# Strassen tiles with A11 and A12 split ahead of the sums, and a pause of the modulation's dot products

## The chip, the cores and the metric

The kernel runs on one core of one Trainium2 chip. The metric is the device time of one execution in microseconds (us); a kernel is judged by the median of several executions. The core has TensorE (PE in the profile, PEld its weight loads), VectorE (DVE), ScalarE (ACT), GpSimd (POOL) and SyncE (SP, which issues the DMAs here).

## The reference, cut to what matters

One inference step of two layers over 128 context and 512 latent tokens, D_MODEL = 1024, D_FF = 2816, all in float32. Each layer is a feed-forward network (FFN), a mixer (attention in layer 0, Fourier mixing in layer 1) and a second FFN, each with a shift, a scale and a gate that come from a modulation:

```python
def _modulation(cond, w, b):
    m = jax.nn.silu(cond) @ w + b            # w: 1024 x 9*1024 per layer
    return jnp.split(m, N_MOD, axis=-1)      # N_MOD = 9

def _swiglu(h, wg, wu, wd):
    return (jax.nn.silu(h @ wg) * (h @ wu)) @ wd

hp = _modulate(_rms(yp, norm_g[l, 0]), mp[0], mp[1])
hs = _modulate(_rms(ys, norm_g[l, 0]), ms[0], ms[1])
yp = yp + 0.5 * mp[2] * _swiglu(hp, ffn_wg[l, 0], ffn_wu[l, 0], ffn_wd[l, 0])
ys = ys + 0.5 * ms[2] * _swiglu(hs, ffn_wg[l, 0], ffn_wu[l, 0], ffn_wd[l, 0])
...                                          # mixer, then the second FFN with m[6], m[7], m[8]
```

There are four FFNs: (0,0), (0,1), (1,0) and (1,1), by layer and place. The last one, (1,1), is followed by the final norm and the outputs.

## The kernel before, in words

**Float32 by three products.** Weights and activations are split into a high part `hi` (cast to fp32r) and a low part `lo` (the rest), and each product is three matmuls, hi by hi, hi by lo and lo by hi (`mm3`, L560, whose three matmuls are L565, L566 and L567). Weights come from HBM raw by SP's queue (`raw`), are cast to `whi` and get their `wlo` by a subtraction. In the first three FFNs ACT casts (L131) and POOL subtracts (L134); in the last FFN ACT casts (L160) and DVE subtracts (L163).

**The first three FFNs** (`ffn`, L874). The 2816 hidden columns are 22 tiles of 128, worked off in chunks: `CHUNKS = (4, 4, 2, 4, 4, 4)`. The tokens are two halves, half 0 of 384 and half 1 of 256 columns. A chunk first makes gate and up of its tiles for both halves (`products`, then the scaling by the norm at L812 and the bias at L822), then `down` (L855) runs the down products of the chunk for half 0 and then for half 1. For each of the eight blocks d of x, `down` takes a PSUM bank, runs the matmuls and has DVE add the product, times the gate, to x (`add_x`, L776). The one-bank PSUM tiles are named `t` (four), the two-bank ones `s` (two). A four-tile chunk has 12 matmuls for each block, the two-tile chunk (chunk 2) has 6, so there a bank is filled in half the time while the add takes as long.

**Modulation.** The 9 vectors of each layer are dot products on DVE that are spread over the FFNs: a task (`mods`, L663) loads 512 KB of w_mod into one of two buffers `wmt` and makes two dots of 128x1024 with it (L681, in the profile CUSTOM_DVE_ANT_0 and a read of the accumulator, out `junk` and `mod`, in `junk<-wmt,crow`). The order of all work is fixed when the kernel is built. The program keeps a clock of its own (`now`, in units it calls ns) that `tick` moves on after each product, and a task goes on when the clock has reached its `wake`. Between two dots the task yields its pace: 2600 for vector 2 of layer 0, 3800 for the other vectors of layer 0, 4300 for layer 1. `need_mod` finishes what a step needs at once.

**The last FFN** (`ffn_last`, L1008) runs chunk 0 as before and chunks 1 to 5 by Strassen's scheme: 18 tiles. A tile's weight is a 2x2 matrix of blocks: rows gate (A11, A12) and up (A21, A22), columns the two halves of K. The 640 tokens are two halves of 320, `first` and `second`. Seven products make the four results instead of eight, each of them 12 matmuls of 128x320, 84 in all (`seven`, L927):

```
P1 = A11 B11   P2 = A12 B21   P6 = S2 T2   P7 = S3 T3   P5 = S1 T1   P3 = S4 B22   P4 = A22 T4
S1 = A21 + A22,  S2 = S1 - A11,  S3 = A11 - A21,  S4 = A12 - S2      (weights)
```

in the order 1, 2, 6, 7, 5, 3, 4 (in a chunk's last tile 1, 2, 6, 5, 7, 3, 4), where the first two products of a tile are drawn between the last ones of the tile before it. The forms of B and T are made once from the norm's output.

**The weights' forms of a tile** are made by a task `load_sums` (L179). It loads two raws of 128x1024, `r1` = (A11, A12) and `r2` = (A21, A22). `take_turn` keeps the tasks in order, and `self.live` lets only two tiles have sums at one time. DVE makes the sums, S1 in the place of A21, ACT casts them (`form`, L192) and DVE makes their low parts (L196). `whole` (L155) makes the high and low part of a whole raw, 128x1024, into a pair of weight buffers:

```python
for c in halves:                                   # L159
    nc.scalar.copy(hi[:, c], raw[:, c])            # L160
yield self.pace
for c in halves:
    nc.vector.tensor_tensor(lo[:, c], raw[:, c], hi[:, c].bitcast(F32), op=ALU.subtract)   # L163
```

`whole(r1)` gives A11 and A12, `whole(r2)` gives S1 and A22. A pair of buffers is taken when `u.room` is above 0 (`take_grain`, six pairs in all); `seven` gives room back after the products that used a pair last, `ffn_last` after the downs. In chunks 1 to 5 `pin` (L996) fixes the program order of PE, DVE and ACT, so each of them works off its instructions as they were written. After a chunk's products its down products run, for half `second` and then `first`.

Of the kernel before, what the change touches and what calls it, by code (L numbers as in the profile page):

```python
# [37 lines left out]
RAW = 1024  # L38
# [49 lines left out]
class Units:  # L88
# [89 lines left out]
    def load_sums(self, ap):  # L178


        k, nc = self.k, self.k.nc
        W = RAW // 2
        r1 = k.raw()
        r2 = k.wide(k.rawpool, "raw", F32, RAW) if self.turn % 2 else k.raw()
        nc.sync.dma_start(r1, ap[:, :RAW])
        nc.sync.dma_start(r2, ap[:, RAW:])
        forms = {}
        tt = nc.vector.tensor_tensor

        def high(name, src):  # L190
            forms[name] = tuple(k.wide(k.fpool, "form", w=W) for _ in range(2))
            nc.scalar.copy(forms[name][0], src)  # L192

        def low(name, src):
            h, l = forms[name]
            tt(l, src, h.bitcast(F32), op=ALU.subtract)  # L196

        yield from self.take_turn(3500)
        while self.live > 1:
            yield 300  # L200
        self.live += 1
        s3, s2 = (k.wide(k.spool2, "s", F32, W) for _ in range(2))
        s1, a11, a12 = r2[:, :W], r1[:, :W], r1[:, W:]
        tt(s3, a11, s1, op=ALU.subtract)
        tt(s1, s1, r2[:, W:], op=ALU.add)
        yield self.pace
        high("S3", s3)
        tt(s2, s1, a11, op=ALU.subtract)
        yield self.pace
        high("S2", s2)  # L210
        low("S3", s3)
        yield self.pace
        low("S2", s2)
        tt(s2, a12, s2, op=ALU.subtract)
        yield self.pace
        high("S4", s2)
        h, l = yield from self.whole(r1)
        forms["A11"], forms["A12"] = (h[:, :W], l[:, :W]), (h[:, W:RAW], l[:, W:RAW])
        low("S4", s2)
        yield self.pace  # L220
        h, l = yield from self.whole(r2)
        forms["S1"], forms["A22"] = (h[:, :W], l[:, :W]), (h[:, W:RAW], l[:, W:RAW])
        yield self.pace
        self.served_one()
        return forms
# [225 lines left out]
class Kern:  # L451
# [422 lines left out]
    def ffn(self, l, i, nrm, nxt, begin=None):  # L874
# [3 lines left out]
        u = self.units  # L878
        for ch, nf in enumerate(CHUNKS):
            last = ch == len(CHUNKS) - 1  # L880
# [9 lines left out]
            first = gm == (0, 2) and ch == 0  # L890
            if not first:
                self.need_mod(gm)
            self.down(wds, gA, 0, gate, nxt if last else None, gm if first else None)
            self.down(wds, gB, 1, gate, nxt if last else None)
            u.prefetch(nf // 2)
# [28 lines left out]
            if not all and steps[1:]:  # L924
                self.staged.append(steps[1:])

    def seven(self, w, forms, G, last):  # L927


        nc = self.nc  # L930
        u = self.units
# [25 lines left out]
        for p in (1, 2, 6, 5, 7, 3, 4) if last else (1, 2, 6, 7, 5, 3, 4):  # L957
            new = ()
# [3 lines left out]
            elif p == 2:  # L962
                c = self.bank()[:, :NH]
                product(c, "A12", "B21", True)
                u.room += 1
                tt(t["s1"], c, t["s1"], op=ALU.add)
                new = (lambda: nc.scalar.activation(t["s1"], t["s1"], AF.Silu),)
            elif p == 6:
# [13 lines left out]
                new = (lambda: tt(gate, t["s3"], gate, op=ALU.mult), *split(gate, "second"))  # L982
            else:
                product(b, "A22", "T4", False)
                u.room += 1
                tt(t["s2"], b, t["s2"], op=ALU.add)
                tt(t["s2"], t["s2"], t["s1"], op=ALU.mult)
                new = split(t["s2"], "first")
# [25 lines left out]
    def ffn_last(self, l, i, nrm, nxt, before_last):  # L1014
# [3 lines left out]
        u = self.units  # L1018
        wide = lambda n: [tuple(self.wide(self.gpool, "g") for _ in range(2)) for _ in range(n)]
        for ch, nf in enumerate(CHUNKS):  # L1020
# [14 lines left out]
            else:  # L1035
# [3 lines left out]
                gs = wide(nf)  # L1039
                old = None  # L1040
                for n, G in enumerate(gs):
                    new = self.seven(u.get(), nrm.forms, G, n == nf - 1)
                    for step in (new, new, old, new, old, new, new) if n else [new] * 5:
                        next(step)
                    old = new
# [585 lines left out]
    def run(self):  # L1631
# [49 lines left out]
        paces = {}  # L1681
        for l in range(2):
            for m in range(2 if l == 0 else 0, NMOD):
                paces[l, m] = 2600 if (l, m) == (0, 2) else (3800 if l == 0 else 4300)
                for d in range(KT):
                    self.modq.append((l, m, d))
        self.modtask = Task(self, self.mods(paces))
# [285 lines left out]
```

## Time and profile before

| | |
|---|---|
| three executions | 2335.15, 2340.88 (median), 2344.72 us |
| profiled execution | 2336.35 us, its span 2334.6 us |
| busy: PE, PEld | 2272.8 us (97%), 2242.2 us (96%) |
| busy: DVE, ACT, POOL | 1609.9 us (69%), 821.4 us (35%), 795.8 us (34%) |
| DMA | 243.92 MB, mean 104 GB/s |

The trace is that of one execution, the profiled one. Times in it count from the span's start. The first three FFNs and the mixers take up to about 1840 us, then come the last FFN with its Strassen chunks and the tail. In a row of the timeline the bracket at its end is the time for which the engine stood idle before the instruction, and what released it. "x12" is a count of instructions or, in a timeline, of equal neighbours that were put together. The page's "granted clock" (PEclk) is the mean of TensorE's clock over a stretch, 1.00 being 2.4 GHz and 0.50 being 1.2 GHz.

### The profile page before, as it was taken

The numbers are of one execution on the slowest core, as the hardware profiler recorded it, in microseconds if no ns is written. First come the engines' busy times: TensorE is split into PE (matmuls) and PEld (weight loads), VectorE is DVE, ScalarE is ACT, GpSimd is POOL, SyncE is SP. The second block draws the span as 40 slices with busy tenths as digits, with TensorE's granted clock in tenths as the row PEclk, the third lists the DMA queues.
The fourth block names the chain that finished last, engine by engine and source line by source line (L and its number), as shares of the span: only waits on it lengthen the run. The fifth ranks groups of instructions, "written<-read, shape, count | busy, mean of one in ns | idle before, by whom it ended". The sixth has DMA issues, their size and how long they took to land.

```text
span 2334.6 us, 38917 instructions
## 1 busy us (share of the span) xinstructions
PE 2272.8 (97%) x15518; PEld 2242.2 (96%) x15518; DVE 1609.9 (69%) x3113; ACT 821.4 (35%) x1725; POOL 795.8 (34%) x655
## 2 busy tenths in 40 slices
PE   8999999999999999999999999999999999999998
PEld 6999999998899999999999999999999999999998
DVE  5867877767677776777666767676457586667665
ACT  4222222254545632222224322222237343333434
POOL 1444444464111244353445533533346530000002
PEclk9999999999999999999999999999999999999999
DMA  8444434421111233444433334443221221322212
GB/s 301 153 128 135 143 127 146 138 76 58 33 42 37 82 100 127 127 144 127 126 118 109 109 121 132 130 132 127 73 75 64 64 73 55 99 63 80 85 46 73
DMA packets 70469, 243.92 MB, mean 104 GB/s; under 512 B 7888, under 2 KB 12688, under 8 KB 70032
## 3 DMA queue, kind: packets, MB, share of 16 engines
q1 hardware_dynamic: 70288, 241.44, 32.3%
q8 instruction: 122, 2.00, 0.4%
q14 instruction: 59, 0.48, 0.1%
HBM read 238.62 MB, written 2.79 MB: 103 GB/s over the span
## 4 chain that ended last, share of the span: by engine, by line
PE 83%; DVE 9%; ACT 3%; issue 2%; POOL 1%; DMA 1%; SPq 0%; POOLq 0%; ACTq 0%; DVEq 0%
PE s L567 16%; PE s L566 16%; PE s L565 16%; PE t L565 11%; PE t L566 11%; PE t L567 11%; DVE x L776 1%; DVE junk L681 1%; DVE b L822 1%; ACT whi L131 1%; PE t L1316 1%; POOL wlo L134 1%; DVE dg L620 0%; DVE sm L1259 0%; DVE b L575 0%
## 5 line engine op out<-in xcount | busy, mean ns | idle before, releaser
L134 POOL TENSOR_TENSOR wlo<-raw,whi 128x512 fp32r<-128x512 f32 x484 | 683.6, 1443 | 991.7 <-ACT whi L131 695.1
L131 ACT CAST whi<-raw 128x1024 fp32r<-128x1024 f32 (+1 forms) x249 | 251.4, 1035 | 508.1 <-PE t L566 293.7
L565 PE MATMUL s<-a,whi 128*128 128x386 f32 (+1 forms) x1188 | 403.1, 340 | 1.7 <-ACT a L286 0.8
L567 PE MATMUL s<-a,wlo 128*128 128x386 f32 (+1 forms) x1188 | 403.1, 339 | 0.1
L566 PE MATMUL s<-a,whi 128*128 128x386 f32 (+1 forms) x1188 | 402.3, 339 | 0.0
L681 DVE CUSTOM_DVE_ANT_0 junk<-wmt,crow 128x1024 f32<-128x1024 f32 x256 | 343.0, 1340 | 2.3 <-ACT crow L1697 0.3
L776 DVE SCALAR_TENSOR_TENSOR x<-t,mod,x 128x128 f32<-128x128 f32 (+2 forms) x640 | 247.9, 423 | 138.5 <-PE t L567 136.4
L565 PE MATMUL s<-b,whi 128*128 128x256 f32 (+1 forms) x1056 | 297.0, 281 | 0.2 <-DVE a L812 0.2
L566 PE MATMUL s<-b,whi 128*128 128x256 f32 (+1 forms) x1056 | 296.8, 281 | 0.0
L567 PE MATMUL s<-b,wlo 128*128 128x256 f32 (+1 forms) x1056 | 296.7, 281 | 0.0
L565 PE MATMUL t<-a,whi 128*128 128x384 f32 (+1 forms) x660 | 225.3, 342 | 3.9 <-ACT a L574 3.0
L565 PE MATMUL t<-b,whi 128*128 128x256 f32 x760 | 216.7, 285 | 10.6 <-DVE x L776 6.3
L565 PEld LDWEIGHTS s<-a,whi 128*128 128x128 f32 x1188 | 224.2, 189 | 2.8 <-ACT a L286 0.9
L567 PEld LDWEIGHTS s<-a,wlo 128*128 128x128 f32 x1188 | 224.2, 189 | 2.2 <-issue 1.6
L566 PEld LDWEIGHTS s<-a,whi 128*128 128x128 f32 x1188 | 224.3, 189 | 1.6 <-issue 1.2
L566 PE MATMUL t<-a,whi 128*128 128x384 f32 (+1 forms) x660 | 224.7, 341 | 0.3 <-DVE a L575 0.2
L567 PE MATMUL t<-a,wlo 128*128 128x384 f32 (+1 forms) x660 | 224.2, 340 | 0.0
L567 PE MATMUL t<-b,wlo 128*128 128x256 f32 x760 | 214.1, 282 | 0.0
L566 PE MATMUL t<-b,whi 128*128 128x256 f32 x760 | 214.1, 282 | 0.0
L565 PEld LDWEIGHTS s<-b,whi 128*128 128x128 f32 x1056 | 199.0, 188 | 0.7 <-issue 0.5
L566 PEld LDWEIGHTS s<-b,whi 128*128 128x128 f32 x1056 | 199.1, 189 | 0.0
L567 PEld LDWEIGHTS s<-b,wlo 128*128 128x128 f32 x1056 | 198.8, 188 | 0.0
(307 smaller groups left out, 4761.4 us busy)
## 6 DMA issues: line engine op xcount, KB each, us to landing
raw<-in_gu SPq DMA_DIRECT2D x176, 512.0 KB, 3.7
wmt<-in_wm SPq DMA_DIRECT2D x134, 512.0 KB, 3.7
raw<-in_dn SPq DMA_DIRECT2D x88, 512.0 KB, 3.7
raw<-in_uq SPq DMA_DIRECT2D x8, 512.0 KB, 3.7
raw<-in_wo SPq DMA_DIRECT2D x8, 512.0 KB, 3.6
raw<-in_fw SPq DMA_DIRECT2D x8, 512.0 KB, 3.8
crow<-in_wm SPq DMA_DIRECT2D x6, 512.0 KB, 5.8
junk<-in_wm SPq DMA_DIRECT2D x4, 512.0 KB, 5.8
```

Source lines behind the costliest of these rows:

```text
L131: nc.scalar.copy(hi, raw[:, :e])
L134: eng.tensor_tensor(lo[:, c], raw[:, c], hi[:, c].bitcast(F32), op=ALU.subtract)
L565: mm(out, wh, xh, start=first and i == 0, stop=False)
L566: mm(out, wh, xl, start=False, stop=False)
L567: mm(out, wl, xh, start=False, stop=last and i == end)
L681: nc.vector.tensor_tensor_reduce(self.junk, raw, self.crow[:, c * D : (c + 1) * D], 1.0, 0.0, ALU.mult, ALU.add, self.mod[l][m][:, d, c : ...
L776: self.mark = self.nc.vector.scalar_tensor_tensor(xd, ps[:, cols], gate[:, d, c : c + 1], xd, ALU.mult, ALU.add)
L822: nc.vector.scalar_tensor_tensor(g[:, cols], up[:, cols], bias[:, 1, c : c + 1], g[:, cols], ALU.add, ALU.mult)
L1316: nc.tensor.transpose(ps[:, o : o + P], ps2[i][:, kt * P : (kt + 1) * P], self.ident)
```

## The change

The change has three parts. In `load_sums`, `whole(r1)` is called as soon as the task has its turn, ahead of the wait for `self.live` and of the sums, and the pause that stood behind A11's split now stands ahead of S4's low part. The room for the weight buffers is counted for that order: `seven` gives one after product 2 only in a chunk's first tile, and two after product 4 but for the last tile, where it gives one. In `ffn`, ahead of the downs of a two-tile chunk, the task of the dots is put off until 20000 on the program's clock from there. And the paces of the dots go from 3800 to 3500 in layer 0 and from 4300 to 4000 in layer 1.

```diff
--- before.py
+++ after.py
@@ -196,6 +196,8 @@
             tt(l, src, h.bitcast(F32), op=ALU.subtract)
 
         yield from self.take_turn(3500)
+        h, l = yield from self.whole(r1)
+        forms["A11"], forms["A12"] = (h[:, :W], l[:, :W]), (h[:, W:RAW], l[:, W:RAW])
         while self.live > 1:
             yield 300
         self.live += 1
@@ -214,10 +216,8 @@
         tt(s2, a12, s2, op=ALU.subtract)
         yield self.pace
         high("S4", s2)
-        h, l = yield from self.whole(r1)
-        forms["A11"], forms["A12"] = (h[:, :W], l[:, :W]), (h[:, W:RAW], l[:, W:RAW])
+        yield self.pace
         low("S4", s2)
-        yield self.pace
         h, l = yield from self.whole(r2)
         forms["S1"], forms["A22"] = (h[:, :W], l[:, :W]), (h[:, W:RAW], l[:, W:RAW])
         yield self.pace
@@ -890,6 +890,8 @@
             first = gm == (0, 2) and ch == 0
             if not first:
                 self.need_mod(gm)
+            if nf == 2:
+                self.modtask.wake = max(self.modtask.wake, self.now + 20000)
             self.down(wds, gA, 0, gate, nxt if last else None, gm if first else None)
             self.down(wds, gB, 1, gate, nxt if last else None)
             u.prefetch(nf // 2)
@@ -924,7 +926,7 @@
             if not all and steps[1:]:
                 self.staged.append(steps[1:])
 
-    def seven(self, w, forms, G, last):
+    def seven(self, w, forms, G, first, last):
 
 
         nc = self.nc
@@ -962,7 +964,7 @@
             elif p == 2:
                 c = self.bank()[:, :NH]
                 product(c, "A12", "B21", True)
-                u.room += 1
+                u.room += first
                 tt(t["s1"], c, t["s1"], op=ALU.add)
                 new = (lambda: nc.scalar.activation(t["s1"], t["s1"], AF.Silu),)
             elif p == 6:
@@ -982,7 +984,7 @@
                 new = (lambda: tt(gate, t["s3"], gate, op=ALU.mult), *split(gate, "second"))
             else:
                 product(b, "A22", "T4", False)
-                u.room += 1
+                u.room += 1 if last else 2
                 tt(t["s2"], b, t["s2"], op=ALU.add)
                 tt(t["s2"], t["s2"], t["s1"], op=ALU.mult)
                 new = split(t["s2"], "first")
@@ -1039,7 +1041,7 @@
                 gs = wide(nf)
                 old = None
                 for n, G in enumerate(gs):
-                    new = self.seven(u.get(), nrm.forms, G, n == nf - 1)
+                    new = self.seven(u.get(), nrm.forms, G, n == 0, n == nf - 1)
                     for step in (new, new, old, new, old, new, new) if n else [new] * 5:
                         next(step)
                     old = new
@@ -1681,7 +1683,7 @@
         paces = {}
         for l in range(2):
             for m in range(2 if l == 0 else 0, NMOD):
-                paces[l, m] = 2600 if (l, m) == (0, 2) else (3800 if l == 0 else 4300)
+                paces[l, m] = 2600 if (l, m) == (0, 2) else (3500 if l == 0 else 4000)
                 for d in range(KT):
                     self.modq.append((l, m, d))
         self.modtask = Task(self, self.mods(paces))
```

What this does to the order of the instructions is shown at three places. Names carry the number of the buffer and of its writing; lines behind L198 are two higher in the kernel after, `ffn`'s and later ones more.

**ACT, the second tile of chunk 1.** The rows begin in the middle of the tile and end where the third tile's first product is drawn in. `raw_3277` is (A11, A12) of the third tile in both, `raw_3278` its other raw. Before:

```order
L948 COPY a_3316_21271<-s_3315_21258 128x320
L967 ACTIVATE a_3316_21271<-a_3316_21271 128x320
L981 ACTIVATE a_3318_21300<-s_3303_21169 128x320
L948 COPY a_3321_21319<-s_3315_21258 128x320
L192 CAST form_3322_21324<-s_3319_21305 128x512
L953 CAST g_3295_21161<-a_3318_21300 128x320
L192 CAST form_3325_21344<-s_3320_21306 128x512
L953 CAST g_3295_21161<-a_3310_21222 128x320
L948 COPY a_3327_21374<-s_3315_21258 128x320
L192 CAST form_3328_21377<-s_3320_21306 128x512
L160 CAST whi_3330_21380<-raw_3277_21020 128x512 x2
L160 CAST whi_3332_21387<-raw_3278_21021 128x512 x2
```

After (`raw_3313` is the fourth tile's (A11, A12), `raw_3248` the second tile's second raw):

```order
L160 CAST whi_3311_21248<-raw_3248_20847 128x512 x2
L160 CAST whi_3316_21262<-raw_3277_21020 128x512 x2
L950 COPY a_3318_21275<-s_3315_21258 128x320
L969 ACTIVATE a_3318_21275<-a_3318_21275 128x320
L983 ACTIVATE a_3320_21306<-s_3295_21152 128x320
L950 COPY a_3323_21325<-s_3315_21258 128x320
L192 CAST form_3324_21330<-s_3321_21311 128x512
L955 CAST g_3287_21144<-a_3320_21306 128x320
L192 CAST form_3327_21350<-s_3322_21312 128x512
L955 CAST g_3287_21144<-a_3304_21208 128x320
L950 COPY a_3329_21380<-s_3315_21258 128x320
L192 CAST form_3330_21383<-s_3322_21312 128x512
```

The casts of `raw_3277` have moved from behind the third tile's last form (`form_3328`) to ahead of the second tile's first copy (`a_3318<-s_3315`), and `raw_3278`'s stay behind the last form.

**DVE, FFN (0,1), the downs of the two-tile chunk.** `x0` to `x7` are the blocks of x; adds of 128x384 are half 0, pairs of 128x128 half 1. ISA rows with `junk` are dots, those with `mod` alone read the sum. Before:

```order
L776 SCALAR_TENSOR_TENSOR x3_78<-t_1991_11506,mod0_8_100,x3_78 128x384
L681 ISA junk_1720_9414,mod1_1_102<-wmt_1721_9415,crow_1719_9413 128x1024
L681 ISA mod1_1_102 128x1
L776 SCALAR_TENSOR_TENSOR x4_79<-s_1992_11514,mod0_8_100,x4_79 128x384
L776 SCALAR_TENSOR_TENSOR x5_80<-s_1993_11526,mod0_8_100,x5_80 128x384
L776 SCALAR_TENSOR_TENSOR x6_81<-t_1994_11534,mod0_8_100,x6_81 128x384
L776 SCALAR_TENSOR_TENSOR x7_82<-t_1995_11545,mod0_8_100,x7_82 128x384
L776 SCALAR_TENSOR_TENSOR x0_75<-t_1996_11553,mod0_8_100,x0_75 128x128 x2
L681 ISA junk_1720_9414,mod1_1_102<-wmt_1721_9415,crow_1719_9413 128x1024
L681 ISA mod1_1_102 128x1
L776 SCALAR_TENSOR_TENSOR x1_76<-t_1997_11562,mod0_8_100,x1_76 128x128 x2
L776 SCALAR_TENSOR_TENSOR x2_77<-t_1998_11573,mod0_8_100,x2_77 128x128 x2
```

After:

```order
L776 SCALAR_TENSOR_TENSOR x3_78<-t_1991_11506,mod0_8_100,x3_78 128x384
L776 SCALAR_TENSOR_TENSOR x4_79<-s_1992_11514,mod0_8_100,x4_79 128x384
L776 SCALAR_TENSOR_TENSOR x5_80<-s_1993_11525,mod0_8_100,x5_80 128x384
L776 SCALAR_TENSOR_TENSOR x6_81<-t_1994_11533,mod0_8_100,x6_81 128x384
L776 SCALAR_TENSOR_TENSOR x7_82<-t_1995_11544,mod0_8_100,x7_82 128x384
L776 SCALAR_TENSOR_TENSOR x0_75<-t_1996_11552,mod0_8_100,x0_75 128x128 x2
L776 SCALAR_TENSOR_TENSOR x1_76<-t_1997_11561,mod0_8_100,x1_76 128x128 x2
L776 SCALAR_TENSOR_TENSOR x2_77<-t_1998_11570,mod0_8_100,x2_77 128x128 x2
L776 SCALAR_TENSOR_TENSOR x3_78<-t_1999_11579,mod0_8_100,x3_78 128x128 x2
L776 SCALAR_TENSOR_TENSOR x4_79<-t_2000_11588,mod0_8_100,x4_79 128x128 x2
L776 SCALAR_TENSOR_TENSOR x5_80<-t_2001_11597,mod0_8_100,x5_80 128x128 x2
L776 SCALAR_TENSOR_TENSOR x6_81<-t_2002_11606,mod0_8_100,x6_81 128x128 x2
```

The two dots between the adds are gone; the next one stands behind the last add of half 1.

**DVE, last FFN, the down of the two-tile chunk.** L204, L205 and L208 (L206, L207 and L210 after) are sums of the next chunk's first tile, L163 the low parts of its A11 and A12, L196 the low part of a form. Pairs of 128x192 and 128x128 are adds of half `second`, 128x320 those of `first`. Before:

```order
L776 SCALAR_TENSOR_TENSOR x5_80<-s_3466_22319,mod1_8_109,x5_80 128x128
L208 TENSOR_TENSOR s_3465_22311<-raw_3440_22142,raw_3439_22141 128x512
L776 SCALAR_TENSOR_TENSOR x6_81<-t_3467_22328,mod1_8_109,x6_81 128x192
L776 SCALAR_TENSOR_TENSOR x6_81<-t_3467_22328,mod1_8_109,x6_81 128x128
L776 SCALAR_TENSOR_TENSOR x7_82<-t_3470_22341,mod1_8_109,x7_82 128x192
L776 SCALAR_TENSOR_TENSOR x7_82<-t_3470_22341,mod1_8_109,x7_82 128x128
L196 TENSOR_TENSOR form_3469_22333<-s_3464_22310,form_3468_22332 128x512
L776 SCALAR_TENSOR_TENSOR x0_75<-t_3471_22350,mod1_8_109,x0_75 128x320
L776 SCALAR_TENSOR_TENSOR x1_76<-t_3474_22362,mod1_8_109,x1_76 128x320
L196 TENSOR_TENSOR form_3473_22355<-s_3465_22311,form_3472_22354 128x512
L214 TENSOR_TENSOR s_3465_22311<-raw_3439_22141,s_3465_22311 128x512
L776 SCALAR_TENSOR_TENSOR x2_77<-t_3475_22370,mod1_8_109,x2_77 128x320
```

After:

```order
L776 SCALAR_TENSOR_TENSOR x7_82<-t_3468_22337,mod1_8_109,x7_82 128x192
L776 SCALAR_TENSOR_TENSOR x7_82<-t_3468_22337,mod1_8_109,x7_82 128x128
L163 TENSOR_TENSOR wlo_3467_22329<-raw_3440_22156,whi_3466_22328 128x512 x2
L206 TENSOR_TENSOR s_3470_22352<-raw_3440_22156,raw_3441_22157 128x512
L207 TENSOR_TENSOR raw_3441_22157<-raw_3441_22157 128x512
L776 SCALAR_TENSOR_TENSOR x0_75<-t_3469_22346,mod1_8_109,x0_75 128x320
L776 SCALAR_TENSOR_TENSOR x1_76<-t_3472_22360,mod1_8_109,x1_76 128x320
L210 TENSOR_TENSOR s_3471_22353<-raw_3441_22157,raw_3440_22156 128x512
L776 SCALAR_TENSOR_TENSOR x2_77<-t_3473_22368,mod1_8_109,x2_77 128x320
L776 SCALAR_TENSOR_TENSOR x3_78<-t_3476_22380,mod1_8_109,x3_78 128x320
L196 TENSOR_TENSOR form_3475_22373<-s_3470_22352,form_3474_22372 128x512
L776 SCALAR_TENSOR_TENSOR x4_79<-t_3477_22388,mod1_8_109,x4_79 128x320
```

Low parts of A11 and A12 and two sums now stand together between the last add of `second` and the first of `first`; before, the sums were drawn between the adds of `second` and the low parts came near the end of `first`.

PE's and POOL's orders are the same before and after. SP's differs in the places of some loads, and there are 256 dots in both.

## Rows read from the trace of the kernel before

**Rows 1.** The page, busy time of each engine (share of the span), number of instructions
```profile
PE 2272.8 (97%) x15518; PEld 2242.2 (96%) x15518; DVE 1609.9 (69%) x3113; ACT 821.4 (35%) x1725; POOL 795.8 (34%) x655
```
**Rows 2.** Waits of PE: line waited for, us in total, times, longest us
```profile
PE s L565 <- ACT whi L160: 12.7, 8, 1.6
PE t L565 <- DVE x L776: 10.4, 11, 2.3
```
**Rows 3.** Timeline of PE at a tile boundary: start, us, engine, line, operation
```profile
1967.76 0.30 PE L567 MATMUL s<-sum,wlo 128*128 128x320 f32 x1
1969.61 0.41 PE L565 MATMUL s<-h,whi 128*128 128x320 f32 x1 [1.55 <-ACT whi L160]
```
**Rows 4.** Timeline of ACT there
```profile
1968.42 0.62 ACT L192 CAST form<-s 128x512 fp32r<-128x512 f32 x1
1968.94 2.18 ACT L160 CAST whi<-raw 128x512 fp32r<-128x512 f32 x4
```
**Rows 5.** Windows: length, busy us (instructions) of each engine, PEclk, DMA share, GB/s
```profile
core 0: us, PE busy (x) PEld busy (x) DVE busy (x) ACT busy (x) POOL busy (x), PEclk, DMA share, GB/s
2068.70:2092.70 24.00, 24.00 (x165) 24.00 (x164) 12.32 (x23) 7.50 (x17) 0.00 (x0) 1.00 0.13 44
1967.76:1971.93 4.17, 2.46 (x16) 1.93 (x14) 3.40 (x7) 3.02 (x6) 0.00 (x0) 1.00 0.08 7
1982.37:1986.58 4.21, 2.44 (x16) 1.92 (x15) 3.39 (x7) 3.81 (x8) 0.00 (x0) 1.00 0.02 2
```
**Rows 6.** Groups of DVE, 1946.77 to 2000.5: count, busy us, mean ns, idle before
```profile
L163 DVE TENSOR_TENSOR wlo<-raw,whi 128x512 fp32r<-128x512 f32 x20 | 12.9, 684 | 1.4 <-ACT whi L160 1.4
L196 DVE TENSOR_TENSOR form<-s,form 128x512 fp32r<-128x512 f32 x7 | 4.8, 683 | 0.0
L954 DVE TENSOR_TENSOR g<-a,g 128x320 fp32r<-128x320 f32 x6 | 2.8, 483 | 0.0
L205 DVE TENSOR_TENSOR raw<-raw 128x512 f32<-128x512 f32 x2 | 1.4, 692 | 0.1
```
**Rows 7.** Windows, two stretches after tile boundaries
```profile
2096.10:2099.40 3.30, 3.30 (x14) 3.30 (x13) 1.60 (x3) 0.46 (x2) 0.00 (x0) 0.50 0.60 171
2276.95:2280.30 3.35, 3.35 (x15) 3.35 (x14) 2.34 (x4) 1.33 (x4) 0.00 (x0) 0.50 0.71 223
```
**Rows 8.** Timelines of PE and DVE, last FFN, down of chunk 2
```profile
2060.92 0.68 DVE L204 TENSOR_TENSOR s<-raw,raw 128x512 f32<-128x512 f32 x1
2064.82 0.38 PE L565 MATMUL t<-g,whi 128*128 128x320 f32 x1 [2.26 <-DVE x L776]
```
**Rows 9.** Windows, half-1 downs of the three two-tile chunks, and 96 gate-up matmuls
```profile
244.46:252.99 8.53, 6.46 (x50) 5.94 (x50) 8.53 (x24) 0.24 (x1) 0.00 (x0) 1.00 0.40 123
1029.20:1037.88 8.68, 6.54 (x50) 5.96 (x49) 8.68 (x25) 0.22 (x1) 0.00 (x0) 1.00 0.42 131
1501.00:1508.43 7.43, 6.29 (x50) 5.91 (x49) 7.43 (x23) 0.23 (x1) 0.00 (x0) 1.00 0.39 133
1009.39:1020.74 11.35, 11.35 (x98) 11.35 (x97) 7.91 (x13) 4.53 (x9) 4.78 (x4) 1.00 0.37 124
```
**Rows 10.** Windows, line L681 alone: DVE busy (dots and their reads), PEclk, DMA, GB/s
```profile
244.46:252.99 8.53, 2.43 (x4) 1.00 0.40 123
1029.20:1037.88 8.68, 2.44 (x4) 1.00 0.42 131
1501.00:1508.43 7.43, 1.29 (x4) 1.00 0.39 133
```
**Rows 11.** Timeline of PE in the second of these downs
```profile
1032.88 0.38 PE L565 MATMUL t<-b,whi 128*128 128x256 f32 x1 [1.74 <-DVE x L776]
```
**Rows 12.** Windows, 60 us of four-tile chunks in FFN (0,0) and FFN (1,0)
```profile
120.00:180.00 60.00, 60.00 (x412) 60.00 (x411) 41.24 (x64) 19.07 (x32) 28.93 (x20) 1.00 0.45 140
1320.00:1380.00 60.00, 60.00 (x416) 60.00 (x415) 45.00 (x77) 13.65 (x24) 21.01 (x16) 1.00 0.40 124
```
**Rows 13.** Dots: duration ns (least/median/longest); and a slow one in the timeline
```profile
L681 DVE CUSTOM_DVE_ANT_0 junk<-wmt,crow x256: 1205/1217/2405, 56.7 to 1642.0; 128x1024 f32<-128x1024 f32 x128
1022.59 2.20 DVE L681 CUSTOM_DVE_ANT_0 junk<-wmt,crow 128x1024 f32<-128x1024 f32 x1
```

## The prediction, made before the change was timed

> **What bounds the kernel now.** I read the engines' busy line first: PE is busy for 2272.8 of 2334.6 us [rows 1], so a change of instructions on another engine is worth what it takes out of PE's 62 us of idle time, out of the slow start after a wait, and out of stretches at the low clock. Then the waits of PE: eight times an `s` product of the last FFN waits for ACT's `whi` of L160, 12.7 us in all, and eleven times a `t` product waits for DVE's `x` of L776, 10.4 us [rows 2]. The timelines show what stands behind each.
>
> At the boundary of two Strassen tiles PE issues the last S1 matmul at 1967.76, and A11's first one only at 1969.61, after 1.55 us of waiting for ACT [rows 3]. ACT casts the form of S4 at 1968.42, and only then, in one run of four casts from 1968.94, A11|A12's and S1|A22's raw weights (L160) [rows 4]. A11|A12 stands behind the sums of its own tile in ACT's order, and so it comes last before it is used first. This happens at tiles 3 and 4 of each of the four four-tile chunks, which are the eight waits.
>
> **Edit 1: A11 and A12 before the sums.** A stretch of 24 us without a stall has 165 matmuls of 128x320 in 24.00 us, 0.146 us each [rows 5]. From the last S1 matmul to the end of A11's twelve are 13 matmuls, 1.90 us. The two boundaries shown took 4.17 and 4.21 us [rows 5], 2.27 and 2.31 over that; the part that is pure wait is 12.7/8 = 1.59. The order now has the two casts of tile T+1's A11|A12 in tile T's first products, ahead of T's first copy out, with five or more products of twelve matmuls (8.8 us) still to run before they are used, and the raw weights' load is the only thing they wait for. I take the whole excess: 8 x 2.29 = 18.3 us. Lower bound, if only the idle time goes: 12.7; upper bound 18.4 (8 x 2.31).
>
> What is late next? In a tile DVE has, by its groups, 4 lows of L163 at 0.684, 3 of L196 at 0.683, 4 sums at 0.692, and seven works of 128x320 at 0.483 or a little over [rows 6]: 2.74 + 2.05 + 2.77 + 3.38 = 10.9 us. That is 89% of a stall-free tile (84 matmuls x 0.146 = 12.3). Nothing is added to it: one pause has moved, and the same 108 casts and 108 lows are there. The sums and S4's low now come later by the 1.4 us of A11's two lows, but they belong to a tile whose first product does not need them: S2 is the third product, S3 the fourth, S4 the sixth. A replay of DVE's and ACT's new order by hand with these durations leaves each form ready 4 us or more before PE wants it, so I cost this at nothing. If that cover were gone it would be the 1.4 us, at each of 18 tiles.
>
> **The clock behind two of the eight.** After two of the eight stalls, but not after the other six, the granted clock is 0.50 (the 1.2 GHz level): 2096.10 to 2099.40 and 2276.95 to 2280.30 [rows 7]. Over 3.30 and 3.35 us that costs half, 1.65 + 1.68 = 3.3 us. Both begin within 4 us of a stall's end, and without the stall I expect none. Bounds: 0, if the drop comes anyway, and 5.0, if the like stretch of 3.3 us after the down of chunk 2 should go as well. I take 3.3. The Trainium skill (TensorE: Matmul & The Clock Gate, "HAM oscillation") says that gaps in PE's work throttle its clock again, and that the phase of this is free of the program; two out of eight like stalls agrees with that. By it the term could as well be 0 or 5.0 in another execution, and the sum 24.0 to 29.0.
>
> **The down of the two-tile chunk in the Strassen stage.** PE waits 2.26 us at 2064.82 for the adds into x there [rows 8]. DVE has three sums among those adds (the first at 2060.92, 0.68 us). In the new order these sums leave their place, but two lows of A11 (1.37 us) and two sums (1.37) stand between the last add of half `second` and the first add of `first`. My replay: the wait at the tenth bank falls from 2.3 to about 0.4, and a new one of about 2.0 appears two banks later, since the bank of the first add comes free only after those four. Gain 0; bounds -2 (one more such wait) and +2.3.
>
> **Edit 2: no dot product in the downs of the two-tile chunks.** In FFNs (0,0), (0,1) and (1,0) the half-1 down of the two-tile chunk has 48 matmuls of 128x256. At 11.35/96 = 0.118 us each (the row of 96 stall-free ones) that is 5.68 us; the three took 8.53, 8.68 and 7.43, an excess of 2.85, 3.00 and 1.75, 7.6 us in all [rows 9]. DVE is busy for every moment of them, and 2.43, 2.44 and 1.29 us of it are dots [rows 10]; PE waits there for the adds, 1.74 us at 1032.88 [rows 11]. The new order has no dot among those adds in any of the three. At (0,0) two dots in place of one now stand just before the second half's scaling (L812), so DVE comes to the adds about 1.2 us late and part of the stall stays, some 1.3 us. Of each place I also leave 0.2 us as the ordinary seam between two groups of matmuls. Gain 7.6 - 1.3 - 0.6 = 5.7 us; lower bound 3 (only (0,1)), upper 7.6.
>
> **Edit 3: the paces, and where the dots go.** There are 256 dots of 1.217 us median before and after. At the pace of 3500 in place of 3800 a four-tile chunk of about 85 us has 24.2 in place of 22.3, so 1.9 x 1.29 (dot and its read) = 2.45 us more on DVE. In 60 us of such a chunk DVE is busy for 41 to 45, and PE for 60.00 of 60.00 [rows 12]: 85 us leave some 20 free, and I cost this at nothing. Its bounds come with the slow rival below. The load of the dot's weights on SP's queue is issued in the task's own step, just as the dot is, so during the pause it is not queued ahead of the raw weights; 12 loads of 512 KB a chunk in place of 11 find a queue whose engines are busy to 0.40 to 0.45 [rows 12]. Where a matrix's modulation is needed early (0,8 at the second FFN's first down) one dot is forced ahead of the first add; six banks cover it.
>
> **Sum.** 18.3 + 3.3 + 0 + 5.7 + 0 = 27.3 us. The profiled execution took 2336.35 us (its span 2334.6 and 1.75 around it), so it would take 2309.0. The median of the runs, 2340.88, lies 4.5 above it; with that, 2313.6. I say 2313.
>
> **Rivals.**
> *DVE becomes the bound of the tile.* For it: 89% by the sum above, a fixed program order, and waits of DVE for ACT and PE within the tile. If a tile took 13.4 us in place of 12.3, 18 tiles lose 19.8, the gain of 21.6 on stalls and clock shrinks to 1.8, and with the dots 7.5 stay: 2336.35 - 7.5 + 4.5 = 2333. Against it: everything PE needs is prepared a tile ahead, so that DVE's waits are not on PE's path. 6%.
> *The change does not do what it says.* The casts stand earlier, but ACT waits in them for a raw buffer that has not landed, and the copies behind it come late in turn. Then only the dots' 5.7 are left: 2330.6 + 4.5 = 2335. Against it: the DMA share in the stall-free stretch is 0.13 [rows 5]. 4%.
> *Slower: dots and weight splits hinder each other in the four-tile chunks.* A dot that runs beside POOL's splits can take 2.20 in place of 1.21 us [rows 13], and POOL is busy there for 21 to 29 of 60 us. If DVE had no free time there and 1.9 dots at 2.28 fell on PE's path, 14 four-tile chunks would lose 4.3 each, 61 us: 2336.35 - 27.3 + 61 + 4.5 = 2374. It decides from (27.3 + 11.7)/14 = 2.8 us lost per chunk. Against it: PE never waits in those stretches, the number of dots is unchanged, and so is the time for which both compete. 3%. The Trainium skill (SBUF — State Buffer, "SBUF: two separate sides") describes this: a DVE operation with two SBUF inputs and a GpSimd operation lock each other out for a whole instruction. The 2.20 us agrees, and by that rule a closer pace speaks against the change, since a split held up by a dot makes its weights late; POOL does nothing in the Strassen stage, so edit 1 is not touched by it.
>
> **How the numbers follow.** The forecast has 87%. Its own range: from 12.7 + 0 + 3 with some loss at chunk 2, about 14 us, to 18.4 + 5.0 + 2.3 + 7.6 = 33; with all at their ends together unlikely, 17 to 31, and the runs of before lie from 2335 to 2345. So 2304 to 2325; to hold 8 in 10 with the rivals, 2303 to 2328. A measurement of this kernel tells 0.5%, 11.7 us, from no change, that is below 2329 or above 2353. Faster 0.87; within 0.5% (two rivals of 2333 and 2335, 10%, and no tail of the forecast worth a count) 0.10; slower 0.03.
>
> **What will show it.** Right: no wait of `s` products for L160 among PE's waits; the boundary of tiles 2 and 3 takes 1.9 us; no low clock between the chunks' downs in the Strassen stage but perhaps after chunk 2; the three half-1 downs take 7.2, 5.9 and 5.9 us; the dots' stretches of 60 us keep PE at 60.00. Wrong: eight waits of 1 us or more for another form (S2, S3 or S4, L196) in their place; an `x` wait of over 3 us in chunk 2; waits for POOL's `wlo` in the first three FFNs.

## The result, and the profile after

The changed kernel takes 2308.29 us (median of 4 executions, 2305.79 to 2310.65); the kernel before 2340.61 with one execution more than shown above (2335.15 to 2344.72). The ratio is 0.9865, with a 95% interval of 0.9848 to 0.9882. The profiled executions are 2336.35 and 2307.57 us, 28.8 apart, with spans of 2334.6 and 2305.8. Forecast were 2313 us and a gain of 27.3 on the profiled execution.

The page after, first part (to be set against [rows 1]):

```profile
PE 2261.2 (98%) x15518; PEld 2235.6 (97%) x15518; DVE 1607.4 (70%) x3113; ACT 820.1 (36%) x1725; POOL 800.0 (35%) x655
```

PE's waits after. The first of the two groups of [rows 2], the eight waits for L160, is no longer in the list; it is now headed by the second:

```profile
PE t L565 <- DVE x L776: 6.4, 8, 1.8
```

PE's order is the same in both kernels, so the start of one and the same matmul can be compared between the two traces. I cut each trace at two matmuls: the first of a group that starts at 1846.81 us before, ahead of the last FFN's chunk 0, and the last down matmul of that FFN's chunk 5, at 2323.28 before.

| stretch | before | after | gain |
|---|---|---|---|
| up to the first cut | 1846.81 | 1840.23 | 6.58 |
| between the cuts (the last FFN) | 476.47 | 453.71 | 22.76 |
| behind the second cut, to the span's end | 11.32 | 11.86 | -0.54 |

**The tile boundary** of [rows 3], in PE's timeline after:

```profile
1961.21 0.31 PE L567 MATMUL s<-sum,wlo 128*128 128x320 f32 x1
1961.36 0.31 PE L565 MATMUL s<-h,whi 128*128 128x320 f32 x1
```

A11's first matmul follows 0.15 us behind the last of S1, at PE's ordinary step. ACT's timeline after shows where the casts of [rows 4] now stand:

```profile
1950.10 2.19 ACT L160 CAST whi<-raw 128x512 fp32r<-128x512 f32 x4
1952.19 0.42 ACT L950 COPY a<-s 128x320 f32<-128x320 f32 x1
...
1961.56 0.43 ACT L950 COPY a<-s 128x320 f32<-128x320 f32 x1 [2.01 <-PE s L567]
1961.88 0.62 ACT L192 CAST form<-s 128x512 fp32r<-128x512 f32 x1
```

The run of four from 1950.10 has the second half of tile 2's forms and, behind it, A11 and A12 of tile 3, 9 us ahead of their use at 1961.36. The last form, at 1961.88, has nothing in front of it now that PE needs.

Windows after, over the boundaries of [rows 5], and over the stretch from the boundary at 2092.72 through the low clock of [rows 7]:

```profile
core 0: us, PE busy (x) PEld busy (x) DVE busy (x) ACT busy (x) POOL busy (x), PEclk, DMA share, GB/s
1961.21:1963.14 1.93, 1.93 (x16) 1.93 (x14) 1.67 (x4) 1.58 (x4) 0.00 (x0) 1.00 0.28 81
1973.59:1975.46 1.87, 1.87 (x15) 1.87 (x14) 1.56 (x4) 1.48 (x4) 0.00 (x0) 1.00 0.29 72
2080.13:2083.80 3.67, 3.67 (x28) 3.67 (x27) 3.34 (x7) 3.27 (x7) 0.00 (x0) 1.00 0.48 143
```

The boundaries take 1.93 and 1.87 us in place of 4.17 and 4.21. The matmuls of the last row started at 2092.72 and 2100.22 before: 7.50 us became 3.67, with the clock at 1.00.

**The half-1 downs** of the two-tile chunks. The first three rows of [rows 9] begin 0.35, 0.15 and 0.12 us ahead of the half's first matmul, so I compare from one and the same matmul here, the last one of half 0, first before and then after:

```profile
244.28:252.99 8.71, 6.64 (x51) 5.96 (x51) 8.71 (x24) 0.24 (x1) 0.00 (x0) 1.00 0.39 122
1029.04:1037.88 8.84, 6.70 (x50) 5.98 (x50) 8.84 (x25) 0.30 (x2) 0.00 (x0) 1.00 0.42 132
1500.95:1508.43 7.48, 6.34 (x50) 5.96 (x50) 7.48 (x23) 0.23 (x1) 0.00 (x0) 1.00 0.39 133
```
```profile
243.07:250.25 7.18, 6.50 (x50) 5.94 (x50) 6.98 (x21) 0.42 (x2) 0.00 (x0) 1.00 0.32 112
1027.61:1033.48 5.87, 5.87 (x50) 5.87 (x50) 5.45 (x17) 0.23 (x1) 0.00 (x0) 1.00 0.24 87
1496.52:1502.35 5.83, 5.83 (x51) 5.83 (x50) 5.50 (x18) 0.23 (x1) 0.00 (x0) 1.00 0.23 80
```

And dots in them after (against [rows 10]; one row is enough, since all three read 0.00 now):

```profile
243.07:250.25 7.18, 0.00 (x0) 1.00 0.32 112
```

They are 1.53, 2.97 and 1.65 us shorter, 6.15 in all. That this is near the 6.58 us up to the first cut is in part chance. The rest of that stretch differs between the two executions by 1 to 2.5 us at several places, in both directions, and it has 17.1 us at the 1.2 GHz level before and 10.2 after. Runs five, six and seven below have the same order as the changed kernel up to there, and the four of them reach the cut between 1838.61 and 1842.73 us. The four-tile windows of [rows 12] are as they were for PE:

```profile
120.00:180.00 60.00, 60.00 (x409) 60.00 (x408) 41.99 (x62) 19.62 (x33) 30.29 (x21) 1.00 0.45 142
1320.00:1380.00 60.00, 60.00 (x406) 60.00 (x405) 45.00 (x81) 13.68 (x23) 21.52 (x15) 1.00 0.38 115
```

**The down of the two-tile chunk in the last FFN.** PE's timeline after has two waits for adds where [rows 8] has one of 2.26 us:

```profile
2051.99 0.39 PE L565 MATMUL t<-g,whi 128*128 128x320 f32 x1 [0.44 <-DVE x L776]
2055.48 0.41 PE L565 MATMUL t<-g,whi 128*128 128x320 f32 x1 [1.49 <-DVE x L776]
```

The whole down, both halves, in windows before and after:

```profile
2053.31:2071.69 18.38, 16.12 (x99) 15.56 (x98) 17.18 (x39) 5.45 (x10) 0.00 (x0) 0.91 0.19 58
2042.59:2059.11 16.52, 14.59 (x99) 14.10 (x98) 15.89 (x38) 4.31 (x8) 0.00 (x0) 1.00 0.22 64
```

### The profile page after: what moved, and what is told of

The parts are those of the page before. It is cut to its first block, busy times and chain, and to the rows that moved or that the text cites. A ratio compares the mean times of both kernels' runs of the same rounds, so it can differ in the third digit from the quotient of the medians.

```text
span 2305.8 us, 38918 instructions
## 1 busy us (share of the span) xinstructions
PE 2261.2 (98%) x15518; PEld 2235.6 (97%) x15518; DVE 1607.4 (70%) x3113; ACT 820.1 (36%) x1725; POOL 800.0 (35%) x655
## 4 chain that ended last, share of the span: by engine, by line
PE 82%; DVE 10%; ACT 3%; issue 2%; POOL 1%; DMA 1%; SPq 0%; POOLq 0%; ACTq 0%; DVEq 0%
PE s L565 16%; PE s L566 16%; PE s L567 16%; PE t L565 10%; PE t L566 10%; PE t L567 10%; DVE x L776 1%; DVE junk L681 1%; DVE b L822 1%; ACT whi L131 1%; POOL wlo L134 1%; PE t L1318 1%; DVE b L287 1%; ACT a L286 1%; DVE dg L620 0%
## 5 line engine op out<-in xcount | busy, mean ns | idle before, releaser
L681 DVE CUSTOM_DVE_ANT_0 junk<-wmt,crow 128x1024 f32<-128x1024 f32 x256 | 345.4, 1349 | 2.7 <-ACT crow L1699 0.6
```

The source lines that it names most:

```text
L681: nc.vector.tensor_tensor_reduce(self.junk, raw, self.crow[:, c * D : (c + 1) * D], 1.0, 0.0, ALU.mult, ALU.add, self.mod[l][m][:, d, c : ...
```

## The experiments

The theory: the eight waits came from the place of A11's split in ACT's and DVE's order, and the dots cost only where they stand in the two-tile downs. Its rivals: DVE as the next bound, dots that only move their cost, and closer paces that cost by themselves.

**One: edit 1 alone** (the changed kernel without the pause, and with the old paces):

```diff
-            if nf == 2:
-                self.modtask.wake = max(self.modtask.wake, self.now + 20000)
-                paces[l, m] = 2600 if (l, m) == (0, 2) else (3500 if l == 0 else 4000)
+                paces[l, m] = 2600 if (l, m) == (0, 2) else (3800 if l == 0 else 4300)
```

> Only edit 1 (A11 and A12 split ahead of the sums, with its room counting); no pause of the dots and the old paces. Theory (the eight waits come from the casts' place in ACT's order, and nothing else becomes late): the eight waits of PE for L160 go, 8 x 2.29 = 18.3 us, with 0 to 5 us of low clock on top, so a span 18 to 23 us below that of before; the first three FFNs as before, within 1 us at their end. Rival (DVE becomes the bound of a tile): waits for forms (L196) or adds in their place, at least 5 us of them, and a span less than 14 us below. Rival (the gain came mostly from the dots): under 12 us.

Measured: 2312.64 us, ratio 0.9896 (0.9877 to 0.9916) to the kernel before (median 2336.6 of 29 executions in these runs, nearer to its profiled one than the three shown first). Between the cuts it takes 453.68 us; the changed kernel takes 453.71. The eight waits are gone, and nothing took their place; its list of PE's waits is headed by the adds, with the dots' stalls still among them:

```profile
PE t L565 <- DVE x L776: 10.3, 13, 1.8
```

So the last FFN's 22.8 us are edit 1's alone. The span, 2314.2, is only 20.4 below, because the stretch up to the first cut took 1.9 us longer in this execution than in the kernel before, where 1 us at most was expected. It has 20.5 us at the 1.2 GHz level there, in place of 17.1; at half the clock the 3.4 more cost up to 1.7 us.

**Two: the pause and the paces alone** (the kernel before with both):

```diff
+            if nf == 2:
+                self.modtask.wake = max(self.modtask.wake, self.now + 20000)
-                paces[l, m] = 2600 if (l, m) == (0, 2) else (3800 if l == 0 else 4300)
+                paces[l, m] = 2600 if (l, m) == (0, 2) else (3500 if l == 0 else 4000)
```

> Only the pause of the dots in the downs of two-tile chunks and the closer paces; the Strassen tiles as before. Theory: the three half-1 downs become 1.6, 3.0 and 1.6 us shorter (6.2 in all, the first keeps a stall of about 0.8), and the eight waits for L160 stay at 12.7 us; a span 5 to 8 us below before, low clock stretches apart. If the low clock after the boundaries is set by the program, it stands at the same two of the eight as in the kernel before; if it is set by a phase that is free of the program, at others or at another number of them. Rival (the dots only move and cost as much elsewhere): the same span as before within 2 us, with new waits in the four-tile chunks.

Measured: 2329.82 us, ratio 0.9972 (0.9961 to 0.9982), 6.8 below that median. The three downs, from the same matmul as above, take what they take in the changed kernel, and the waits for L160 stand unchanged in its list:

```profile
242.56:249.69 7.13, 6.49 (x50) 5.93 (x50) 6.93 (x21) 0.37 (x2) 0.00 (x0) 1.00 0.36 113
1025.28:1031.15 5.87, 5.87 (x50) 5.87 (x50) 5.46 (x17) 0.23 (x1) 0.00 (x0) 1.00 0.26 89
1494.19:1500.02 5.83, 5.83 (x51) 5.83 (x50) 5.53 (x18) 0.23 (x1) 0.00 (x0) 1.00 0.24 87
```
```profile
PE s L565 <- ACT whi L160: 12.7, 8, 1.6
```

The two halves add up in the stretches that they reach: 22.8 us in the last FFN (run one) and 6.2 in the three downs here make 29.0, and the profiled executions lie 28.8 apart. By medians, against the same 2336.6 us, they gain 24.0 and 6.8, and the whole 28.3. The low clock answers the other question. Here it stands behind one of the eight boundaries, another than in the kernel before (behind the second of chunk 1; 3.40 us of which most is at 1.2 GHz), and behind neither of the two of [rows 7]:

```profile
1977.20:1980.60 3.40, 3.40 (x16) 3.40 (x16) 2.70 (x5) 2.42 (x5) 0.00 (x0) 0.55 0.62 169
```

**Three: the paces alone.**

```diff
-                paces[l, m] = 2600 if (l, m) == (0, 2) else (3800 if l == 0 else 4300)
+                paces[l, m] = 2600 if (l, m) == (0, 2) else (3500 if l == 0 else 4000)
```

> Only the closer paces (3500 and 4000), no pause, Strassen tiles as before. Theory (dots cost nothing in the four-tile chunks and what they cost in the two-tile downs goes by how many fall there): at most 2 us either way against before, with stalls in the three half-1 downs of 1 to 3 us each still there. Rival (closer dots cost time, up to 14 chunks x some tenths of a us): 3 us or more above before, spread over the four-tile chunks; then the pause is worth more than the 6 us seen.

Measured: 2340.9 us, ratio 1.0013 (1.0000 to 1.0025): no gain, at most a small loss. Its span, 2334.5, is that of before. Its windows over the three downs, again from the last matmul of half 0, and those of its dots there:

```profile
243.29:253.44 10.15, 6.61 (x50) 5.93 (x50) 10.15 (x30) 0.40 (x2) 0.00 (x0) 1.00 0.40 127
1028.39:1038.20 9.81, 7.77 (x50) 7.35 (x50) 9.47 (x25) 0.23 (x1) 0.00 (x0) 0.83 0.30 104
1501.41:1509.72 8.31, 6.58 (x50) 5.92 (x50) 8.31 (x22) 0.23 (x1) 0.00 (x0) 1.00 0.43 146
```
```profile
243.29:253.44 10.15, 3.31 (x6) 1.00 0.40 127
1028.39:1038.20 9.81, 3.21 (x6) 0.83 0.30 104
1501.41:1509.72 8.31, 2.43 (x4) 1.00 0.43 146
```

8.95 us of dots and reads stand in them, and before 6.22 in the same stretches; they take 28.27 us in place of 25.03, 3.2 more. Up to 1.7 of that is low clock in the second (9.81 us at 0.83). The four-tile chunks are not longer: outside these downs and the mixers, the FFNs' matmuls keep step with those of before to about 0.2 us. So the cost is where the theory had it; the median, 4.3 us above that of before, is more than its 2 us. The gain of edits 2 and 3 needs the pause. The pause under the old paces was not tried, so what the paces add to it is open; by this run it is not speed.

**Four: A11's split one step earlier, not a whole tile** (the kernel before with):

```diff
         tt(s2, a12, s2, op=ALU.subtract)
-        yield self.pace
-        high("S4", s2)
         h, l = yield from self.whole(r1)
         forms["A11"], forms["A12"] = (h[:, :W], l[:, :W]), (h[:, W:RAW], l[:, W:RAW])
+        high("S4", s2)
+        yield self.pace
         low("S4", s2)
         yield self.pace
```

> The kernel before, with A11 and A12 split just ahead of S4's form instead of just behind it: one step of the task (1400 on the program's clock) earlier and not a whole tile. On ACT the casts then stand ahead of the second tile's last copy and of S4's cast. Theory (what counts is the place in ACT's order): the casts are done some 1.5 to 2 us earlier, so the waits at the eight boundaries fall from 1.59 to 0.6 us or less each and the span by 12 to 18 us, low clock apart. Rival (a whole tile ahead is needed, since the sums before it hold DVE and ACT): the waits stay at 1 us or more and the span falls by less than 6 us.

Measured: 2327.62 us, ratio 0.9961 (0.9951 to 0.9972), a gain of 9.0, and 8.75 between the cuts (467.72). Of the 8.75, 3.4 are the two low stretches behind boundaries, which this execution does not have. So the theory's figures fell. The rival's held, waits of 1 us or more and, low clock apart, 5.3 us; its reason, that the sums hold DVE and ACT, turned out right for DVE alone. PE's waits for L163 before and then here, its PE at the boundary, and ACT and DVE there:

```profile
PE s L567 <- DVE wlo L163: 1.3, 8, 0.2
```
```profile
PE s L567 <- DVE wlo L163: 11.0, 8, 1.4
```
```profile
1975.31 0.42 PE L567 MATMUL s<-h,wlo 128*128 128x320 f32 x1 [1.34 <-DVE wlo L163]
```
```profile
1971.60 1.14 ACT L160 CAST whi<-raw 128x512 fp32r<-128x512 f32 x2
```
```profile
1972.84 0.69 DVE L214 TENSOR_TENSOR s<-raw,s 128x512 f32<-128x512 f32 x1
1973.44 0.48 DVE L954 TENSOR_TENSOR g<-a,g 128x320 fp32r<-128x320 f32 x1
1974.16 0.49 DVE L990 TENSOR_TENSOR a<-t,a 128x320 f32<-128x320 f32 x1 [0.23 <-ACT a L948]
1974.57 1.28 DVE L163 TENSOR_TENSOR wlo<-raw,whi 128x512 fp32r<-128x512 f32 x2
```

The casts are done by 1972.74, ahead of A11's first matmul at 1973.50, and no product waits for them. The low parts come one pace (1400) behind in the task and behind three other works on DVE, and PE now waits for these, 1.34 us in place of 1.55 for ACT and 0.16 for DVE. So ACT's order was only the first of two places that were late, and both had to move. What moved in the change was the whole split, with a tile of lead.

**Five and six: more work for DVE in each Strassen tile** (the changed kernel with S3 made twice, and four times):

```diff
         tt(s3, a11, s1, op=ALU.subtract)
+        tt(s3, a11, s1, op=ALU.subtract)        # one in five, three in six
```

> The changed kernel with one more sum per Strassen tile on DVE (S3 made twice, into the same place): 18 x 0.69 = 12.4 us more work for DVE. Theory (a tile leaves DVE 12.3 - 10.9 = 1.4 us): no new wait of PE in the four-tile chunks and no more than 1 us more at the two-tile chunk's down, so from the first Strassen tile to the end within 2 us of the changed kernel, low clock apart. Rival (DVE has in truth nothing to spare in a tile, because it also waits for ACT and PE): some 0.7 us per tile, 10 us or more.

> The changed kernel with three more sums per Strassen tile on DVE (S3 made four times): 2.07 us per tile, 0.7 over the 1.4 that are free by the sum of the groups. Theory (DVE is then the bound of a tile): waits of PE for forms or lows appear in the four-tile chunks, growing from tile to tile as DVE falls behind by 0.7 each, 4 to 12 us in all from the first Strassen tile to the end, and 1 to 4 us more at the two-tile chunk's down. Rival (the forms' lead of 4 us and the downs, where DVE is free, take it up): under 4 us in all. Rival (DVE had less to spare): 20 us or more.

Measured: 2309.55 us, ratio 0.9871 (0.9848 to 0.9895), and 2313.88 us, ratio 0.9890 (0.9867 to 0.9914); the ratios of runs five to eight are to 7 other executions of the kernel before, median 2337.03. Between the cuts 455.11 and 460.60 us, 1.40 and 6.89 more than the changed kernel. In both all of it lies in the two-tile chunk (35.71 and 41.20 us from a matmul amid its products to the end of its down, in place of 34.29). The other chunks are within 0.03 us of the changed kernel. Five's 1.40 us, half of them ahead of the down and half in it, are one extra sum of 0.69 for each of the chunk's two tiles. Six, over 60 us of chunk 1 and over the stretch at the low clock in the two-tile chunk's down, and PE's waits in that chunk:

```profile
1940.00:2000.00 60.00, 60.00 (x412) 60.00 (x411) 52.68 (x97) 29.27 (x61) 0.00 (x0) 1.00 0.28 88
2057.10:2063.90 6.80, 5.71 (x21) 5.71 (x22) 6.14 (x12) 1.31 (x3) 0.00 (x0) 0.50 0.01 2
```
```profile
2041.26 0.42 PE L568 MATMUL t<-h,whi 128*128 128x320 f32 x1 [2.33 <-DVE a L995]
2052.54 0.38 PE L568 MATMUL t<-g,whi 128*128 128x320 f32 x1 [0.44 <-DVE x L779]
2058.20 0.63 PE L568 MATMUL t<-g,whi 128*128 128x320 f32 x1 [3.67 <-DVE x L779]
```

So "DVE becomes the bound of the tile" falls for the four-tile chunks, even at 2.07 us more per tile. I put that down to the 28 us of downs, in which the forms of later tiles are made as well, while my sum had charged them all to the tiles; no run varies the downs. For the two-tile chunk it is right: DVE is its bound, and in six the long wait also ends in the low clock, 5.7 us of matmuls at half speed, some 2.8 of the 6.89 us. The other 4.0 are about its six extra sums (4.1). That six's total lies in the theory's 4 to 12 us is luck, since none of it came where the theory put it.

**Seven: the sums of the next tile later in that down** (the changed kernel with, in `load_sums` behind A11's split, and in `ffn_last` around the downs):

```diff
+        if self.soft:
+            yield self.soft
...
+            u.soft = 2500 if nf == 2 else 0
             for H in (0, 1) if ch == 0 or last else ("second", "first"):
...
+            u.soft = 0
```

> The changed kernel, but in the down of the Strassen stage's two-tile chunk the task waits 2500 on the program's clock between A11's split and the sums of the next tile, so that two of the sums come behind four adds of half 'first' and not ahead of them. Theory (PE's second wait there is the place of two lows and two sums ahead of the first add): that wait falls from 1.65 to about 0.3 us, the other stays at 0.60, the next tile's forms are still in time; 1.4 us less than the changed kernel there, too small for the medians. Rival (the sums are needed at once): a wait of 1 us or more for forms in the next chunk's first tile, and no gain.

Measured: 2307.71 us, ratio 0.9860 (0.9832 to 0.9888); 452.35 us between the cuts, 1.36 less than the changed kernel. PE's waits in that down are now:

```profile
2054.48 0.39 PE L568 MATMUL t<-g,whi 128*128 128x320 f32 x1 [0.42 <-DVE x L779]
2056.64 0.41 PE L568 MATMUL t<-g,whi 128*128 128x320 f32 x1 [0.16 <-DVE x L779]
```

The second wait was the place of the lows and sums, as read from the order. The version beats both kernels in this stage; against the changed kernel its median (0.6 us lower) shows nothing.

**Eight: a closer pace still** (the changed kernel):

```diff
-                paces[l, m] = 2600 if (l, m) == (0, 2) else (3500 if l == 0 else 4000)
+                paces[l, m] = 2600 if (l, m) == (0, 2) else 2600
```

> The changed kernel with a pace of 2600 in place of 3500 and 4000 for every vector: 33 dots in a four-tile chunk of 85 us in place of 24 or 21, some 11 us more of DVE's 20 free ones, until a layer's dots are done. Theory (dots cost nothing where PE is the bound): PE stays without new waits in the four-tile chunks, within 2 us of the changed kernel at the end of the first three FFNs, low clock apart. Rival (dots and POOL's splits hinder each other, or dots come ahead of adds and scalings that PE waits for): waits of PE for POOL's weights, for the scaled activations or for adds, 5 us or more.

Measured: 2309.30 us, ratio 0.9870 (0.9845 to 0.9894). Up to the first cut 1841.31 us in place of 1840.23; its early four-tile window has PE at 60.00 while DVE is busy for 49.28 and POOL for 31.62:

```profile
120.00:180.00 60.00, 60.00 (x411) 60.00 (x411) 49.28 (x76) 19.35 (x32) 31.62 (x21) 1.00 0.53 166
```

Two short waits are new, in the downs of (0,1)'s two-tile chunk, one for L812's work and one for an add:

```profile
1023.55 0.45 PE L565 MATMUL s<-a,whi 128*128 128x384 f32 x1 [0.64 <-DVE b L812]
1029.72 0.39 PE L565 MATMUL t<-b,whi 128*128 128x256 f32 x1 [0.60 <-DVE x L776]
```

Both halves of that down take 16.64 us in place of 14.17, so the closer pace costs 2.5 us there. That the cut comes only 1.1 us later says little, since executions of one order differ by 4 us up to it. In the four-tile chunks, where PE is the bound, the dots cost nothing that can be seen.

## Why the prediction was right

*A11's split: 18.3 us forecast.* The two boundaries shown gained 2.24 and 2.34 us. Over the 43 matmuls from the last one ahead of each of the eight on, PE takes 71.87 us before and 50.48 after, 21.4 less; 3.4 of these are the two low stretches, and 18.0 are left for the boundaries. Run one shows that it is this edit. The cause was told by half: I named ACT's order alone, and run four shows that DVE's low parts stood as late. The idle time too was 14.0 us and not 12.7, with the 1.3 us of waits for L163.

*The clock: 3.3 us forecast.* Both stretches of [rows 7] went, and so did the third, behind the down of chunk 2, which I had kept at 0 and had as the upper bound. In executions with eight waits the low clock stood behind two of eight (before), one of eight (two), one of eight (three, the first of chunk 3 again) and none (four, with waits of 1.4 us). Without the waits it stood behind none in the changed kernel and in runs one, five, six, seven and eight. So the term goes with the waits, but its size was that of one execution, and that it came out is in part luck. That the program alone does not set the low clock is seen where the order is one and the same: up to the first cut the changed kernel and runs five, six and seven have 10.2, 20.5, 10.2 and 13.7 us of it. The Trainium skill (TensorE: Matmul & The Clock Gate, "What's actually happening") states that the phase is free of the program; these counts agree. Its section "HAM oscillation", which the prediction names, is about waits for DMA of several us; that a wait as short as 1.6 us can be followed by the low clock is what these traces show, and not that section.

*The down of chunk 2: 0 forecast.* It took 18.38 us before and takes 16.52 after, 1.86 less. The waits did nearly what was replayed, 2.26 us before and 0.44 + 1.49 after. Run two has the wait of before, 2.27 us, with no low clock behind it, and takes 17.20 us there:

```profile
2046.18:2063.38 17.20, 14.86 (x99) 14.04 (x98) 16.57 (x39) 5.11 (x10) 0.00 (x0) 1.00 0.20 62
```

So 1.2 of the gain are low clock and 0.7 the order. A new wait of 0.15 us ahead of the down took 0.3 back.

*The dots: 5.7 us forecast, 6.15 measured*, 1.53, 2.97 and 1.65. From the last matmul of half 0 the downs now take 7.18, 5.87 and 5.83 us, which are the 7.2, 5.9 and 5.9 of the forecast, the stall of 1.3 at (0,0) among them. What I had too small is the side of before: the windows of [rows 9] begin 0.18, 0.16 and 0.05 us behind that matmul, and have 24.64 us in all where 25.03 are to be compared.

*The paces: 0 forecast.* PE keeps 60.00 of 60.00 in the four-tile chunks, and run eight shows the same with DVE busier by 7 us. Run three shows that closer dots also fall more often into the two-tile downs when nothing holds them out, which I had not charged to the paces, and the pause hid.

*The rivals.* That the casts would wait in their new place falls by run one, DVE as the bound by runs five and six but for the two-tile chunk. For the slower one, 2.8 us lost in each four-tile chunk was named as the point from which it decides; run eight, with 19 dots in the 60 us from 120 in place of 13, loses nothing there that can be seen. Its dots were all done by 1308 us (1653 in the changed kernel), so the later four-tile chunks do not test it.

*The sum: 27.3 forecast, 28.8 measured* on the profiled executions. The four terms that I had at 18.3, 3.3, 0 and 5.7 came to 18.0, 3.4, 1.6 and 6.15 us. The step that failed most in us was the last one: I added the 4.5 us by which the first three executions' median lay above the profiled one. Over 29 executions that median is 2336.6, within 0.3 us of the profiled execution, and the changed kernel's profiled run too lies within 0.8 us of its median. Without that step the forecast would have been 2309.

## What to carry to other kernels

Where an engine's program order is fixed, an operand that the next tile needs first must not stand behind work that it needs later; read for each such operand all the engines that make it, since moving one of two late halves gives the wait to the other. Work that is free on average is paid for in the one short stage where its engine is the bound, so it pays to hold it out of that stage and nothing else. And a gain that is summed from one trace is best set against that execution's own time.

## What the runs showed that was not expected

With the same order on PE, executions agree between the cuts far more closely than their times do: 453.71 and 453.68 us for the changed kernel and run one, and within 0.03 us in every chunk that an edit does not reach, while the times of a kernel's executions spread over 2 to 12 us. Part of that spread is the clock: the 29 executions of the kernel before have a mean granted clock from 0.989 to 0.995, and the one at 0.989 is the longest (2344.66 us). A wait in PE costs more than its idle time: 1.59 us of waiting for ACT and 0.16 for DVE came to 2.3 us at each boundary. And a wait is not always followed by the low clock: behind the 2.3 us in the down of chunk 2 it stood in two executions (before and run three) and not in a third (run two).
